# AdaLN modulation as one fp32 product on the array's column quarters, and the token mixers' two-operand elementwise work on VectorE

## The chip, the cores and the metric

The kernel runs on one core of a Trainium2 chip. The metric is the device time of one execution in microseconds (us). TensorE (PE in the profile) multiplies matrices, VectorE (DVE), ScalarE (ACT) and GpSimd (POOL) work on elements, and SyncE (SP) issues most DMA transfers. Each engine runs its instructions in the order in which they stand in its own queue.

## The reference

One layer of a hybrid decoder in fp32, on a prompt of 1024 tokens and 8 samples of 4 tokens. The conditioning vectors `c` (one for the prompt and one for each sample, nine in all) give scale, shift and gate of both sub-layers:

```
mod = silu(c) @ w_ada + b_ada                       # 1024 -> 6*1024, for 9 rows
sh1, sc1, gt1, sh2, sc2, gt2 = split(mod, 6)
h = rmsnorm(x, norm1) * (1 + sc1) + sh1
y = token_mixers(h)     # p = h @ w_in; RWKV-7 on p[:1792], HGRN2 on the rest; @ w_out
x = x + gt1 * y
h = rmsnorm(x, norm2) * (1 + sc2) + sh2
x = x + gt2 * (square(relu(h @ w_up)) @ w_down)
```

Among the elementwise work of the mixers are, in RWKV, `kk = k * k_k`, `k * (1 + (a-1) k_a)`, the bonus `sum(r * k * r_k) * v` and `+ lnx_b`.

## The kernel before

A matrix product in fp32 precision is made of three fp32r products. `load_w` brings a piece of a weight (`wraw`, 128x512), ACT copies it to fp32r (`whi`, L172), an elementwise engine subtracts that from the weight (`wlo`, L176), and `gemm` multiplies the high part of the weight by the high and the low part of the activation, and the low part by the high (L186 to L188). For the input projection L176 stands on DVE for 99 pieces and on POOL for 45; 96 more come back from DRAM as they were written at first use.

The stages, with their times in the profiled execution:

- **Opening, 0 to 55 us.** `x0`, the first quarter of the tokens with the samples (288 columns), is loaded and then the 8 halves of four blocks of `w_ada` (`wa`, 1 MB each), which give scale and shift of the first norm. `ada_block` splits each 128x512 piece on ACT (`wah`, L235) and DVE (`wal`, L236; two pieces on POOL) and multiplies it by `c_hl`, the split conditioning (L238, L239), into `ps_adb`. `adt` copies that out of PSUM, `two9` adds the halves and transposes (L244, `ps_ada`), and `mod` gets the bias. `modulate0` then scales and shifts `x0` (L306, L307, L310) and splits it into `h` and `l`.
- **Mixers, 55 to about 935 us.** 120 units of input projection, 24 matmuls each, evacuated into RWKV parts (`praw`, `xsh` by L585 to L591, sent to DRAM as `x_d`) or HGRN parts. Between them run nine RWKV groups (`rwkv`, three in flight at different steps), the HGRN heads (`hgrn_mix`), the norms of the other quarters (`sqa`, L264), and 16 calls of `ada_pair`, which make the rest of `mod`, two of its 48 pieces per call, in the way of `ada_block` (`wada`, `wahi` L214, `walo` L215, matmuls L218 and L219). About half of the pairs come in the last 85 us, when no projection is left.
- **Output projection and MLP, 935 to 1746 us.** POOL has nothing to do there.

In an RWKV group `X` is read back from `x_d`; L687 on POOL makes `kk` from it, and L690, L691 and L715 the other two-operand products. DVE makes `bo` in the same tile as `kk` (L720), four small DMAs of SP carry it into `bot`, and POOL adds `lnx_b` there (L727). The triangular inverse of the group is a chain of small steps on POOL (L825, L827), on `iat`, which comes back from DRAM.

A scheduler decides at build time, by its own estimates of durations, in which order each engine's instructions stand. A change of engines or instructions therefore reorders the mixers as a whole.

## Time and profile before

| | us |
|---|---|
| median of 3 runs (1748.58 to 1761.52) | 1751.42 |
| profiled execution | 1748.32 |
| its span, from the first instruction to the last | 1746.4 |
| PE busy | 1601.1 |
| DVE busy | 1277.9 |
| ACT busy | 903.4 |
| POOL busy | 466.7 |

The busy times are of the whole span. The stages have different limits, so what a change is worth is read stage by stage. POOL's whole work lies before 935 us.

### The profile page before, as it was taken

How to read it: one execution, taken by the hardware profiler on the slowest of the kernel's cores; microseconds unless marked ns; L12 is line 12 of the kernel's file. 1: busy time of each engine (PE TensorE's matmuls, PEld its weight loads, DVE VectorE, ACT ScalarE, POOL GpSimd, SP SyncE). 2: the span in 40 equal slices, each digit the busy share in tenths (PEclk: the TensorE clock that was granted, in tenths of full speed). 3: DMA queues.
4: the chain of work that ended last, by engine and by line, in shares of the span. 5: the costliest groups of instructions: out<-in, count | busy, mean ns of one | idle time of the engine just before them, and what ended most of it. 6: DMA issues, size and time to landing. Idle time of an engine off the chain costs nothing.

```text
span 1746.4 us, 38086 instructions
## 1 busy us (share of the span) xinstructions
PE 1601.1 (92%) x14224; PEld 1491.0 (85%) x14224; DVE 1277.9 (73%) x2735; ACT 903.4 (52%) x1861; POOL 466.7 (27%) x977
## 2 busy tenths in 40 slices
PE   6787998999899999899988997999999999999895
PEld 3777887787788888788867997999999999999895
DVE  7777878786655657566776669655655869798998
ACT  6446543446466665657654446455444554443351
POOL 3755738546351625436340000000000000000000
PEclk9899889999889999998988998999999999999997
DMA  7676675866677775765547533443333442324122
GB/s 261 191 226 220 200 231 155 289 211 186 180 230 219 217 227 167 220 183 156 160 143 250 202 129 116 142 140 102 105 104 111 154 147 94 111 87 139 35 75 100
DMA packets 216168, 288.66 MB, mean 165 GB/s; under 512 B 48264, under 2 KB 119304, under 8 KB 212912
## 3 DMA queue, kind: packets, MB, share of 16 engines
q1 hardware_dynamic: 198112, 263.16, 47.7%
q10 hardware_dynamic: 17776, 23.01, 3.9%
q8 instruction: 112, 1.84, 0.4%
q14 instruction: 72, 0.59, 0.1%
q0 software_dynamic: 96, 0.07, 0.0%
HBM read 225.64 MB, written 58.29 MB: 163 GB/s over the span
## 4 chain that ended last, share of the span: by engine, by line
PE 60%; DVE 17%; DMA 8%; ACT 5%; issue 4%; POOL 4%; SPq 1%; ACTq 0%; DVEq 0%; POOLq 0%
PE ps_g L1097 36%; PE ps_in L186 3%; PE ps_in L187 3%; PE ps_in L188 3%; DMA wraw<-w_in 2%; POOL itmp L825 2%; POOL ixt L827 2%; PE ps_A L755 1%; PE ps_l L429 1%; DVE acc L1384 1%; DMA x<-xT 1%; DVE wlo L1086 1%; DVE bl L1380 1%; DVE wlo L176 1%; DMA iat<-at_d 1%
## 5 line engine op out<-in xcount | busy, mean ns | idle before, releaser
L1097 PE MATMUL ps_g<-bh,whi 128*128 128x264 f32 x1792 | 370.7, 287 | 13.6 <-ACT whi L1085 8.5
L1097 PE MATMUL ps_g<-bh,wlo 128*128 128x264 f32 x1792 | 369.9, 287 | 9.0 <-DVE wlo L1086 9.0
L1097 PE MATMUL ps_g<-bl,whi 128*128 128x264 f32 x1792 | 371.0, 287 | 1.4 <-DVE bl L1380 1.4
L186 PE MATMUL ps_in<-h,whi 128*128 128x256 f32 (+1 forms) x960 | 292.2, 306 | 17.8 <-ACT psmp L583 8.4
L1097 PEld LDWEIGHTS ps_g<-bh,whi 128*128 128x128 f32 x1792 | 282.6, 190 | 14.6 <-ACT whi L1085 8.7
L1097 PEld LDWEIGHTS ps_g<-bh,wlo 128*128 128x128 f32 x1792 | 281.1, 190 | 9.7 <-DVE wlo L1086 9.7
L187 PE MATMUL ps_in<-l,whi 128*128 128x256 f32 (+1 forms) x960 | 286.7, 299 | 3.0 <-DVE l L1064 2.1
L188 PE MATMUL ps_in<-h,wlo 128*128 128x256 f32 (+1 forms) x960 | 285.7, 299 | 3.8 <-DVE wlo L176 3.7
L1097 PEld LDWEIGHTS ps_g<-bl,whi 128*128 128x128 f32 x1792 | 281.9, 190 | 1.6 <-DVE bl L1380 1.6
L186 PEld LDWEIGHTS ps_in<-h,whi 128*128 128x128 f32 x960 | 189.6, 198 | 32.2 <-ACT psmp L583 10.2
L172 ACT ACTIVATE whi<-wraw 128x512 fp32r<-128x512 f32 x240 | 147.6, 627 | 111.8 <-PE ps_in L187 55.9
L187 PEld LDWEIGHTS ps_in<-l,whi 128*128 128x128 f32 x960 | 190.2, 198 | 7.6 <-DVE l L1064 2.5
L188 PEld LDWEIGHTS ps_in<-h,wlo 128*128 128x128 f32 x960 | 189.4, 198 | 7.7 <-DVE wlo L176 4.8
L1085 ACT ACTIVATE whi<-wd 128x512 fp32r<-128x512 f32 x112 | 69.4, 630 | 163.9 <-PE ps_g L1097 127.5
L1085 ACT ACTIVATE whi<-wu 128x512 fp32r<-128x512 f32 x112 | 70.3, 632 | 145.6 <-PE ps_g L1097 140.2
L825 POOL TENSOR_TENSOR itmp<-ixt,iat 128x60 f32<-128x60 f32 (+24 forms) x248 | 92.0, 371 | 65.8 <-DMA iat<-at_d 49.4
L1086 DVE TENSOR_TENSOR wlo<-wu,whi 128x512 fp32r<-128x512 f32 x112 | 76.5, 687 | 39.3 <-ACT whi L1085 39.1
L176 DVE TENSOR_TENSOR wlo<-wraw,whi 128x512 fp32r<-128x512 f32 x99 | 77.4, 786 | 34.5 <-ACT whi L172 34.3
L827 POOL TENSOR_TENSOR ixt<-ixt,itmp 128x60 f32<-128x60 f32 (+24 forms) x248 | 90.3, 364 | 17.2
L1086 DVE TENSOR_TENSOR wlo<-wd,whi 128x512 fp32r<-128x512 f32 x112 | 76.0, 685 | 13.6 <-ACT whi L1085 13.5
L1380 DVE TENSOR_TENSOR bl<-u,bh 128x528 fp32r<-128x528 f32 x112 | 73.8, 702 | 2.3 <-ACT bh L1379 2.3
L176 POOL TENSOR_TENSOR wlo<-wraw,whi 128x512 fp32r<-128x512 f32 x45 | 60.7, 1352 | 25.8 <-ACT whi L172 19.8
(399 smaller groups left out, 3239.3 us busy)
## 6 DMA issues: line engine op xcount, KB each, us to landing
wraw<-w_in SPq DMA_DIRECT2D x240, 256.0 KB, 3.9
wlo<-wlo_d SPq DMA_DIRECT2D x96, 256.0 KB, 4.0
wu<-w_up SPq DMA_DIRECT2D x74, 256.0 KB, 2.8
u<-u_d SPq DMA_DIRECT2D x16, 1056.0 KB, 4.9
wada<-w_ada SPq DMA_DIRECT2D x64, 256.0 KB, 3.8
wd<-w_down SPq DMA_DIRECT2D x64, 256.0 KB, 2.6
u_d<-c SPq DMA_DIRECT2D x48, 264.0 KB, 3.0
wa<-w_ada SPq DMA_DIRECT2D x8, 1024.0 KB, 14.4
```

The source lines that it names most:

```text
L172: nc.scalar.activation(hi, raw, AF.Copy)
L176: eng[i].tensor_tensor(lo, raw, hi.bitcast(F32), op=ALU.subtract)
L186: nc.tensor.matmul(out, lhsT=wh, rhs=ah, start=first and k == 0, stop=False)
L187: nc.tensor.matmul(out, lhsT=wh, rhs=al, start=False, stop=False)
L188: nc.tensor.matmul(out, lhsT=wl, rhs=ah, start=False, stop=last and k == len(w) - 1)
L429: nc.tensor.matmul(ps[:, c, :], lhsT=z[:, cs], rhs=zc[:, :, 1, :], start=True, stop=True)
L825: G.tensor_tensor(tm, xt[:, 0:ns, j:j + 1].to_broadcast([P, ns, w]), at[:, j, j + 1:32].unsqueeze(1).to_broadcast([P, ns, w]), op=ALU.mult)
L827: G.tensor_tensor(dst, dst, tm, op=ALU.add)
L1085: self.nc.scalar.activation(hi, src, AF.Copy)
L1086: self.nc.vector.tensor_tensor(lo, src, hi.bitcast(F32), op=ALU.subtract)
L1097: nc.tensor.matmul(out[c], lhsT=w[x][:, k, :], rhs=a[y][:, k, c * 264:c * 264 + 264], start=first and k == 0 and j == 0, stop=last and k = ...
L1380: V.tensor_tensor(lo[:, k, :], src[:, k, :], hi[:, k, :].bitcast(F32), op=ALU.subtract)
```

## The change

It has two parts.

AdaLN: no split any more. The conditioning `c_silu` is padded with zeros from 9 to 32 columns, each piece of `w_ada` goes into one fp32 matmul as it comes from DRAM, and the product of input block `k` is written to PSUM partitions `32*(k%4)` and up, so that four blocks in turn use the four column quarters of the array. `ps_adb` and `ps_adp` so hold four partial sums, and `four9` (128x9) adds them while it transposes. The copies L235 and L214 and the subtractions L236 and L215 are gone, and with them the tiles `wah` and `wal`.

Elementwise work: fifteen kinds of two-operand instructions of the mixers and the opening go from POOL to DVE (among them the 45 subtractions of L176, `sqa`, L1630 on `x0`, and of an RWKV group L687, L690, L691, L715 and L727). The inverses, the sample part of `modulate0`, copies and memsets stay on POOL.

```diff
@@ -190,59 +187,48 @@
-        self.csr = pool.tile([P, KT, 2, NSEQ], F32R, name="c_hl")
-        nc.vector.tensor_copy(self.csr[:, :, 0, :], self.cs)
-        nc.vector.tensor_tensor(self.csr[:, :, 1, :], self.cs, self.csr[:, :, 0, :].bitcast(F32), op=ALU.subtract)
+        self.cs = pool.tile([P, KT, 32], F32, name="c_silu")
+        nc.vector.memset(self.cs, 0.0)
+        nc.vector.tensor_tensor(self.cs[:, :, 0:NSEQ], c, s, op=ALU.mult)
+
+    def ada_product(self, ps, k, w):
+
+        g = 32 * (k % 4)
+        self.nc.tensor.matmul(ps[g:g + 32], lhsT=self.cs[:, k, :], rhs=w, start=k < 4, stop=k >= KT - 4, skip_group_check=True)
+
+    def ada_mod(self, m, n, ps, pool, pp, tag):
+
+        nc = self.nc
+        t = pool.tile([P, n, P], F32, tag="adt", name="adt", bufs=1)
+        nc.scalar.activation(t, ps, AF.Copy)
+        for i in range(n):
+            ps = pp.tile([P, NSEQ], F32, tag=tag, name="ps_ada")
+            nc.tensor.matmul(ps, lhsT=t[:, i, :], rhs=self.four9, start=True, stop=True)
+            nc.vector.tensor_scalar(self.mod[:, m + i, :], ps, self.vec("b_ada", m + i), None, op0=ALU.add)
...
     def ada_pair(self, m, wpool, pool, pp, tag):
-        nc = self.nc
-        ps = pp.tile([2 * NSEQ, 2, P], F32, tag=tag, name="ps_adp")
+        ps = pp.tile([P, 2, P], F32, tag=tag, name="ps_adp")
         for k0 in range(0, KT, 2):
             raw = wpool.tile([P, 2, 2, P], F32, tag="wraw", name="wada", bufs=WB[0])
-            nc.sync.dma_start(raw, self.io["w_ada"][m:m + 2, :, k0:k0 + 2, :].rearrange("m p k c -> p m k c"))
-            hi = wpool.tile([P, 2, 2, P], F32R, tag="whi", name="wahi", bufs=WB[1])
-            lo = wpool.tile([P, 2, 2, P], F32R, tag="wlo", name="walo", bufs=WB[1])
-            nc.scalar.activation(hi, raw, AF.Copy)
-            nc.vector.tensor_tensor(lo, raw, hi.bitcast(F32), op=ALU.subtract)
+            self.nc.sync.dma_start(raw, self.io["w_ada"][m:m + 2, :, k0:k0 + 2, :].rearrange("m p k c -> p m k c"))
             for k in range(2):
-                c = self.csr[:, k0 + k]
-                nc.tensor.matmul(ps, lhsT=c.rearrange("p two s -> p (two s)"), rhs=hi[:, :, k, :], start=k0 + k == 0, stop=False)
-                nc.tensor.matmul(ps[:NSEQ], lhsT=c[:, 0, :], rhs=lo[:, :, k, :], start=False, stop=k0 + k == KT - 1)
+                self.ada_product(ps, k0 + k, raw[:, :, k, :])
+        self.ada_mod(m, 2, ps, pool, pp, tag)
...
     def ada_block(self, b, raw, pool, pg, ph):
 
-        nc = self.nc
-        ps = pg.tile([2 * NSEQ, 4, P], F32, tag="g", name="ps_adb")
-        for kh in range(2):
-            hi = pool.tile([P, 4, 4, P], F32R, tag="wah", name="wah", bufs=2)
-            lo = pool.tile([P, 4, 4, P], F32R, tag="wal", name="wal", bufs=2)
-            for k in range(4):
-                nc.scalar.activation(hi[:, :, k], raw[kh][:, :, k], AF.Copy)
-                (nc.gpsimd if b >= AB and k == AK else nc.vector).tensor_tensor(lo[:, :, k], raw[kh][:, :, k], hi[:, :, k].bitcast(F32), op=ALU.subtract)
-                c = self.csr[:, kh * 4 + k]
-                nc.tensor.matmul(ps, lhsT=c.rearrange("p two s -> p (two s)"), rhs=hi[:, :, k, :], start=kh == 0 and k == 0, stop=False)
-                nc.tensor.matmul(ps[:NSEQ], lhsT=c[:, 0, :], rhs=lo[:, :, k, :], start=False, stop=kh == 1 and k == 3)
+        ps = pg.tile([P, 4, P], F32, tag="g", name="ps_adb")
+        for k in range(KT):
+            self.ada_product(ps, k, raw[k // 4][:, :, k % 4, :])
+        self.ada_mod(4 * b, 4, ps, pool, ph, "h")
...
-        G.tensor_tensor(r, k, r, op=ALU.mult)
+        V.tensor_tensor(r, k, r, op=ALU.mult)
...
-                G.tensor_tensor(qs, qe[:, cols[j]].unsqueeze(1).to_broadcast([P, 4, SC]), self.tokm[:, gs, :], op=ALU.mult)
+                V.tensor_tensor(qs, qe[:, cols[j]].unsqueeze(1).to_broadcast([P, 4, SC]), self.tokm[:, gs, :], op=ALU.mult)
-                G.tensor_tensor(s0, s0, el[:, gs, :].to_broadcast([P, 4, P]), op=ALU.mult)
+                V.tensor_tensor(s0, s0, el[:, gs, :].to_broadcast([P, 4, P]), op=ALU.mult)
                 vm = pool.tile([SC, 4, P], F32, tag="hvm", name="hvm", bufs=B_hvm)
-                G.tensor_tensor(vm, vt[:, j, :].unsqueeze(1).to_broadcast([SC, 4, P]),
+                V.tensor_tensor(vm, vt[:, j, :].unsqueeze(1).to_broadcast([SC, 4, P]),
...
         kk = t4("kk")
-        G.tensor_tensor(kk, k, bc4(self.vec("k_k")), op=ALU.mult)
+        V.tensor_tensor(kk, k, bc4(self.vec("k_k")), op=ALU.mult)
...
-        G.tensor_tensor(k, k, cs, op=ALU.mult)
-        G.tensor_tensor(a, a, sg, op=ALU.mult)
+        V.tensor_tensor(k, k, cs, op=ALU.mult)
+        V.tensor_tensor(a, a, sg, op=ALU.mult)
...
-        G.tensor_tensor(cs, r, k, op=ALU.mult)
+        V.tensor_tensor(cs, r, k, op=ALU.mult)
         bo = kk
...
-        G.tensor_tensor(bt, bt, bc4(self.vec("lnx_b")), op=ALU.add)
+        V.tensor_tensor(bt, bt, bc4(self.vec("lnx_b")), op=ALU.add)
...
-                G.tensor_tensor(ax[:, j], ar[:, j, 0, y, :32].unsqueeze(1).to_broadcast([P, NS, 32]), self.tokm, op=ALU.mult)
+                V.tensor_tensor(ax[:, j], ar[:, j, 0, y, :32].unsqueeze(1).to_broadcast([P, NS, 32]), self.tokm, op=ALU.mult)
...
-                G.tensor_tensor(rm, R[:, j, h, :].unsqueeze(1).to_broadcast([P, NS, 64]),
+                V.tensor_tensor(rm, R[:, j, h, :].unsqueeze(1).to_broadcast([P, NS, 64]),
...
-            G.tensor_tensor(oc, oc, rs[:, c].unsqueeze(2).to_broadcast([P, 4, 64]), op=ALU.mult)
+            V.tensor_tensor(oc, oc, rs[:, c].unsqueeze(2).to_broadcast([P, 4, 64]), op=ALU.mult)
...
-                            self.square_add(hp, x(k), acc, k == 0, nc.gpsimd)
+                            self.square_add(hp, x(k), acc, k == 0, nc.vector)
...
-                    (nc.gpsimd if k in XM else nc.vector).tensor_tensor(x0[:, k, :], x0[:, k, :], r0, op=ALU.mult)
+                    nc.vector.tensor_tensor(x0[:, k, :], x0[:, k, :], r0, op=ALU.mult)
...
-                V, G = nc.vector, nc.gpsimd
-                w = self.load_w(wp, io["w_in"][m], wlo_d.get(m), m in seen, (V, V) if m in seen else [(G, G), (G, V)][self.nw % 2])
+                V = nc.vector
+                w = self.load_w(wp, io["w_in"][m], wlo_d.get(m), m in seen, (V, V))
...
-    o["two9"] = np.concatenate([np.eye(NSEQ, dtype=np.float32)] * 2)
+    o["two9"] = np.concatenate([np.eye(32, NSEQ, dtype=np.float32)] * 4)
```

The first place is PE's order at the end of the opening; `ps_adb` is the product with `w_ada`, `ps_ada` its transposition into `mod`, and `ps_in` the first unit of the projection. Before:

```order
L238 MATMUL ps_adb<-wah,c_hl 18x512
L239 MATMUL ps_adb<-wal,c_hl 9x512
L244 MATMUL ps_ada<-two_77,adt 128x9 x4
L186 MATMUL ps_in<-h_388,whi 128x288 x2
L187 MATMUL ps_in<-l_389,whi 128x288
L188 MATMUL ps_in<-h_388,wlo 128x288
```

Now:

```order
L213 MATMUL ps_ada<-four_74,adt 128x9 x2
L204 MATMUL ps_adb<-wa_138,c_silu 32x512 x4
L204 MATMUL ps_adb<-wa_141,c_silu 32x512 x4
L213 MATMUL ps_ada<-four_74,adt 128x9 x4
L204 MATMUL ps_adb<-wa_142,c_silu 32x512 x4
L213 MATMUL ps_ada<-four_74,adt 128x9 x4
L183 MATMUL ps_in<-h_273,whi 128x288
L184 MATMUL ps_in<-l_274,whi 128x288
```

The products with `wa` now stand in fours, one for each quarter, and wait for the load alone; the pairs that waited for ACT's copy and DVE's subtraction are gone.

The second place is an RWKV group in the middle of the mixers, where `bot` and the `kk` of the next group are made. Before, POOL's queue:

```order
L1014 TENSOR_TENSOR oc<-oc,ors 128x256 x2
L727 TENSOR_TENSOR bot<-bot,vecs 128x512
L687 TENSOR_TENSOR kk<-X,vecs 128x512
L438 TENSOR_TENSOR hr<-hk,hr 128x256
L383 MEMSET hr 128x128
L825 TENSOR_TENSOR itmp<-ixt,iat 128x31
```

Now DVE's queue (L706 is `bo`, L713 `bot`, L673 `kk`; the lines between them are of HGRN heads and of another group):

```order
L706 TENSOR_TENSOR kk<-X,ps_bo 128x512
L368 COPY hr<-hf 128x128
L373 TENSOR_TENSOR hf<-hf 128x128
L713 TENSOR_TENSOR bot<-bot,vecs 128x512
L438 SCALAR_TENSOR_TENSOR hst<-hst,hf,ps_s 128x128 x2
L350 TENSOR_SCALAR hf<-hsig,fs,fb 128x256
L365 TENSOR_TENSOR hz<-hq,hf 128x64x2
L371 TENSOR_TENSOR hz<-hk,hr 128x64x2
L372 TENSOR_TENSOR hr<-hr,hf 128x64x2
L744 TENSOR_TENSOR Aa<-ps_A,amask 128x256
```

The two instructions that wait for DMAs now stand in DVE's queue, `bot` two short instructions behind the `bo` that its DMAs carry, and `kk` some ten further on.

## Rows read from the trace of the kernel before

**Rows 1.** Windows by stage; after each bracket its length, busy times, clock, DMA.

```profile
core 0: us, PE busy (x) PEld busy (x) DVE busy (x) ACT busy (x) POOL busy (x), PEclk, DMA share, GB/s
0.00:55.00 55.00, 36.08 (x132) 18.87 (x133) 42.33 (x89) 31.82 (x66) 24.24 (x33) 0.84 0.66 232
55.00:112.00 57.00, 48.09 (x336) 45.87 (x335) 42.73 (x71) 23.12 (x60) 43.77 (x83) 0.97 0.63 192
112.00:400.00 288.00, 257.55 (x2101) 222.65 (x2099) 227.46 (x517) 144.03 (x345) 162.71 (x286) 0.94 0.71 224
400.00:850.00 450.00, 417.83 (x4559) 377.98 (x4559) 287.19 (x816) 275.02 (x614) 202.93 (x509) 0.94 0.66 197
850.00:935.00 85.00, 67.86 (x871) 54.80 (x869) 64.77 (x194) 50.70 (x121) 33.01 (x70) 0.88 0.52 156
935.00:1746.00 811.00, 773.67 (x6237) 770.84 (x6236) 613.45 (x1052) 378.75 (x656) 0.00 (x0) 0.97 0.36 122
```

**Rows 2.** Windows, 33 to 43 us, same columns.

```profile
33.00:43.00 10.00, 9.22 (x34) 3.60 (x33) 9.34 (x18) 6.00 (x12) 4.88 (x4) 0.78 0.01 3
```

**Rows 3.** Timeline of the opening: start, length, what [idle before, releaser].

```profile
42.29 0.59 ACT L241 ACTIVATE adt<-ps_adb 18x512 f32<-18x512 f32 x1 [0.33 <-PE ps_adb L239]
...
51.07 0.61 PE L187 MATMUL ps_in<-l,whi 128*128 128x288 f32 x1 [2.14 <-DVE l L1064]
```

**Rows 4.** Groups by line: busy us, mean ns of one | idle before them.

```profile
L176 DVE TENSOR_TENSOR wlo<-wraw,whi 128x512 fp32r<-128x512 f32 x99 | 77.4, 786 | 34.5 <-ACT whi L172 34.3
L1086 DVE TENSOR_TENSOR wlo<-wu,whi 128x512 fp32r<-128x512 f32 x112 | 76.5, 687 | 39.3 <-ACT whi L1085 39.1
L176 POOL TENSOR_TENSOR wlo<-wraw,whi 128x512 fp32r<-128x512 f32 x45 | 60.7, 1352 | 25.8 <-ACT whi L172 19.8 <-DMA wraw<-w_in 2.6 <-PE ps_in L188 2.3
L215 DVE TENSOR_TENSOR walo<-wada,wahi 128x512 fp32r<-128x512 f32 x64 | 46.3, 731 | 20.7 <-ACT wahi L214 20.1 <-ACT hkt L402 0.2
L214 ACT ACTIVATE wahi<-wada 128x512 fp32r<-128x512 f32 x64 | 39.4, 628 | 31.5 <-DMA wada<-w_ada 12.1 <-PE ps_in L187 11.5 <-PE ps_adp L218 3.7
L586 DVE SCALAR_TENSOR_TENSOR xsh<-dsh,vecs,praw 128x256 f32<-128x256 f32 x56 | 37.7, 673 | 0.6
```

**Rows 5.** Line L586 and line L825: duration in ns, min/median/max.

```profile
L586 DVE SCALAR_TENSOR_TENSOR xsh<-dsh,vecs,praw x56: 383/484/1557, 59.5 to 468.8; 128x256 f32<-128x256 f32 x56
...
L825 POOL TENSOR_TENSOR itmp<-ixt,iat x248: 202/308/1402, 254.7 to 893.4; 128x60 f32<-128x60 f32 x12, 128x54 f32<-128x54 f32 x8, 128x66 f32<-128x66 f32 x8, 128x28 f32<-128x28 f32 x8
```

**Rows 6.** PE's timeline: fp32r products of a pair, an fp32 matmul, fp32 on quarters.

```profile
164.53 0.28 PE L218 MATMUL ps_adp<-wahi,c_hl 128*18 128x256 f32 x1
164.65 0.28 PE L219 MATMUL ps_adp<-walo,c_hl 128*9 128x256 f32 x1
...
271.95 1.07 PE L996 MATMUL ps_Ss<-rm,btm 128*64 128x512 f32 x2
272.86 0.34 PE L422 MATMUL ps_l<-hz 128*64 128x64 f32 x3
...
300.54 0.25 PE L986 MATMUL ps_Os<-R,Ar 128*32 128x64 f32 x2
300.56 0.25 PE L981 MATMUL ps_Os<-R,Ar 128*32 128x64 f32 x2
...
300.64 0.23 PE L981 MATMUL ps_Os<-R,Ar 128*32 128x64 f32 x2
```

**Rows 7.** POOL's waits: us in total, times, longest.

```profile
POOL bot L727 <- DMA bot<-kk: 61.7, 8, 20.9
...
POOL kk L687 <- DMA X<-x_d: 21.0, 8, 6.0
```

**Rows 8.** Issues of the four bot DMAs in 400 to 850 us, and to landing.

```profile
L726 SPq DMA_DIRECT2D bot<-kk x24: 590/629/1101, 471.0 to 846.8; - x24
...
DMA to landing us min/median/max: 2.0/3.0/5.5
```

**Rows 9.** The chain of waits from 850 to 935 us, by line.

```profile
by line: POOL itmp L825 16.5%; POOL ixt L827 14.9%; issue 8.2%; PE ps_adp L218 4.1%; PE ps_adp L219 4.1%; DMA wo<-w_out 4.0%; DMA at_d<-Aa 3.7%; DMA iat<-at_d 3.3%; PE ps_ada L224 3.0%; PE ps_l L429 2.9%; DMA XT<-xt_d 2.5%; DMA xt_d<-ixt 2.
```

More of the change, by code (lines that the diff above doesn't have):

```diff
@@ L84 @@
 PSB = 2, 2, 1
-AK = 3
 LSQ = ()
@@ L90 @@
 HP0 = 1000
-AB = 3
-XM = (0, 1, 2, 3, 4, 5, 6, 7)
 EPS = 1e-6
@@ L151, in consts @@
         nc.gpsimd.dma_start(self.ident, io["ident"])
-        self.two9 = pool.tile([2 * NSEQ, NSEQ], F32, name="two9")
-        nc.gpsimd.dma_start(self.two9, io["two9"])
+        self.four9 = pool.tile([P, NSEQ], F32, name="four9")
+        nc.gpsimd.dma_start(self.four9, io["two9"])
         self.seqm = pool.tile([P, NS], F32, name="seqm")
@@ L192, in silu_c @@
         nc = self.nc
+        self.mod = pool.tile([P, 48, NSEQ], F32, name="mod")
         c = pool.tile([P, KT, NSEQ], F32, name="c_in")
         nc.scalar.dma_start(c, self.io["cT"])
-        s = pool.tile([P, KT, NSEQ], F32, name="c_sig")
+        s = self.mod[:, 0:KT, :]
         nc.scalar.activation(s, c, AF.Tanh, scale=0.5)
         nc.vector.tensor_scalar(s, s, 0.5, 0.5, op0=ALU.mult, op1=ALU.add)
-        self.cs = pool.tile([P, KT, NSEQ], F32, name="c_silu")
-        nc.vector.tensor_tensor(self.cs, c, s, op=ALU.mult)
@@ L200, in silu_c @@
-        self.csr = pool.tile([P, KT, 2, NSEQ], F32R, name="c_hl")
-        nc.vector.tensor_copy(self.csr[:, :, 0, :], self.cs)
-        nc.vector.tensor_tensor(self.csr[:, :, 1, :], self.cs, self.csr[:, :, 0, :].bitcast(F32), op=ALU.subtract)
-        self.mod = pool.tile([P, 48, NSEQ], F32, name="mod")
+        self.cs = pool.tile([P, KT, 32], F32, name="c_silu")
[4 more added lines that the diff above has]
+        self.nc.tensor.matmul(ps[g:g + 32], lhsT=self.cs[:, k, :], rhs=w, start=k < 4, stop=k >= KT - 4, skip_group_check=True)
@@ L220, in ada_pair @@
-        t = pool.tile([2 * NSEQ, 2, P], F32, tag="adt", name="adt", bufs=1)
-        nc.scalar.activation(t, ps, AF.Copy)
-        for i in range(2):
-            ps = pp.tile([P, NSEQ], F32, tag=tag, name="ps_ada")
-            nc.tensor.matmul(ps, lhsT=t[:, i, :], rhs=self.two9, start=True, stop=True)
-            nc.vector.tensor_scalar(self.mod[:, m + i, :], ps, self.vec("b_ada", m + i), None, op0=ALU.add)
-    def ada_block(self, b, raw, pool, pg, ph):
-        nc = self.nc
-        ps = pg.tile([2 * NSEQ, 4, P], F32, tag="g", name="ps_adb")
-        for kh in range(2):
-            hi = pool.tile([P, 4, 4, P], F32R, tag="wah", name="wah", bufs=2)
-            lo = pool.tile([P, 4, 4, P], F32R, tag="wal", name="wal", bufs=2)
-            for k in range(4):
-                nc.scalar.activation(hi[:, :, k], raw[kh][:, :, k], AF.Copy)
-                (nc.gpsimd if b >= AB and k == AK else nc.vector).tensor_tensor(lo[:, :, k], raw[kh][:, :, k], hi[:, :, k].bitcast(F32), op=ALU.subtract)
-                c = self.csr[:, kh * 4 + k]
-                nc.tensor.matmul(ps, lhsT=c.rearrange("p two s -> p (two s)"), rhs=hi[:, :, k, :], start=kh == 0 and k == 0, stop=False)
-                nc.tensor.matmul(ps[:NSEQ], lhsT=c[:, 0, :], rhs=lo[:, :, k, :], start=False, stop=kh == 1 and k == 3)
-        t = pool.tile([2 * NSEQ, 4, P], F32, tag="adt", name="adt", bufs=1)
-        nc.scalar.activation(t, ps, AF.Copy)
-        for m in range(4):
-            ps = ph.tile([P, NSEQ], F32, tag="h", name="ps_ada")
-            nc.tensor.matmul(ps, lhsT=t[:, m, :], rhs=self.two9, start=True, stop=True)
-            nc.vector.tensor_scalar(self.mod[:, 4 * b + m, :], ps, self.vec("b_ada", 4 * b + m), None, op0=ALU.add)
```

## The prediction

> **What bounds the kernel now.** The first view is the windows by stage [rows 1]. From 935 us on PE is busy 774 of 811 us, POOL not at all, and no line of the change runs there: that stage stays as it is. What can move lies in the first 935 us, and each stage there has its own limit. In the opening DVE is the fullest engine (42 of 55 us). In the first units (55 to 112 us) POOL has 44 of 57 us and DVE 43. From 112 to 400 us PE has 258 of 288 us, DVE 227, POOL 163. From 400 to 850 us PE has 418 of 450 us, and DVE, at 64%, isn't the bound. In the last 85 us no engine is full: the time is a chain. PE's busy time counts overlapping records, so there is slack behind it.
>
> The second view is the opening close up. From 33 to 43 us the DMA engines are idle (share 0.01) while DVE is busy 9.3 of 10 us [rows 2]: all of `wa` has landed and the split is what is being waited for. The last `ps_adb` is copied out at 42.29 us, and the first unit runs on from 51.07 us [rows 3].
>
> The third view is durations. The same subtraction of 128x512 takes 687 ns on DVE in the MLP, where POOL is silent, 786 ns in the mixers, and 1352 ns on POOL [rows 4]. L586 has a median of 484 ns, a mean of 673 and a longest of 1557 [rows 4, 5]; L825 on POOL runs from 202 to 1402 ns with a median of 308. Both engines stretch each other: some instructions wait a whole instruction of the other.
>
> **The change part by part.**
>
> *Opening.* The 32 copies on ACT and 32 subtractions go. After the last load (33 us at the latest) there remain one group of four fp32 products, then what follows 42.29 us today. An fp32 matmul of 512 columns takes some 0.91 us to the start of the next [rows 6]. That makes 33 + 1 + 8.8 (from 42.29 to 51.07) = 42.8 us for the first unit: 8 us gained, one end. The other: of those 8.8 us most is scaling, shifting and splitting both halves of `x0` on a DVE that POOL stretches, and the first half needs only the blocks that land before the last. If it is ready when the last `ps_ada` is, about 2 us behind the product, PE starts near 35 us: 16 us gained. The norm on `x0`, now on DVE, comes while the loads still run, and 8 instructions below 0.69 us are 5.5 us at most, under the loads. In SP's queue nine small constants now stand ahead of the first `w_in` pieces; their transfer falls into the stretch in which the DMA engines were idle, but the first `wraw` may come 2 to 3 us later than the product, so I take **-13** (-16 to -6).
>
> *First units, 55 to 112 us.* POOL, the fullest engine, gives its subtractions and squares to DVE at half the price each (687 against 1352). DVE gets about 16 us more and loses the stretch (L586's mean to its median is 28% of its time, so some 12 us of 43). **-3** (-8 to +3).
>
> *112 to 400 us.* Here DVE becomes the tight engine. Of POOL's 163 us I reckon about 100 as moved work (inverses begin only at 254.7 us [rows 5], and copies and memsets are small); at 687/1352 that is 51 us on DVE. It loses a share of its stretch, between the 13% of L176 (786 to 687) and the 28% of L586: 227 x 0.15 = 34, of which some two thirds go with the moved work, 22 us. So 227 + 51 - 22 = 256 of 288 us, 89% against 79%. If DVE keeps all its idle time of 61 us, the stage ends 29 us later; if that idle time was only waiting for others (PE is at 89% as well), it ends no later, and shorter steps of the groups gain up to 10. Nearer to the second, because DVE's largest wait at L176 is for ACT [rows 4], which gets no more work: **+6** (-10 to +25).
>
> *400 to 850 us.* About half of the 16 pairs are here. A pair has 16 fp32r matmuls at 0.12 us [rows 6], 1.9 us; now it has 8 fp32 matmuls of 256 columns, 0.46 us each if alone (half of 0.91), 0.46 for four if they run at once. That four run at once the trace shows: on four quarters the records of L986 and L981 start at 300.54 and 300.56 us and the second pass follows at 300.64 [rows 6], where four in series, at 64/512 of 0.91 us each, would need 0.46 us. So a pair costs 0.9 instead of 1.9 us, 16 us less in all sixteen, half of them here. ACT loses 39 us of copies in all [rows 4], DVE 46 of subtractions, of which half here; DVE gets back some 30 us of moved work. DVE stays near 64%, PE has 8 us less: **-5** (-12 to +30, for the wait in the first rival).
>
> The Trainium skill, "TensorEngine Tiling (Array Packing)", section Key Properties, says that switching the tiling mode drains the TensorEngine. In the rows a record of L218 lasts 0.28 us at a spacing of 0.12 [rows 6]; if each switch cost those 0.16 us, at both ends of some 45 runs of quarter matmuls, it would be 14 us of PE, and with half of it on the path the sum below would be 7 us nearer to zero. No row shows such a gap at a change of the columns, so I take nothing for it.
>
> *Last 85 us.* The chain of waits has 8.2% in L218 and L219 and 31.4% in the inverse on POOL [rows 9]. Half of the pairs stand here: their DVE and ACT work of about 20 us each goes. The chain's 7 us in L218 and L219 fall to half; the inverse, at 26.7 us on the chain, has less DVE beside it and may fall toward its median. What is late next is `at_d` and back, which stays. **-6** (-11 to 0).
>
> That the remaining POOL work gains is supported by the Trainium skill, "SBUF — State Buffer", section "SBUF: two separate sides": a VectorE instruction with two SBUF inputs and a GpSimd instruction that reads SBUF lock each other out for a whole instruction. The trace agrees (202 to 1402 ns at L825). By the same rule every moved instruction now holds up the inverses that stay, so the gain in the middle stage is less than POOL's relief.
>
> Sum: -13 - 3 + 6 - 5 - 6 = **-21**. Against the profiled execution of 1748.3 us (span 1746.4) that is 1727; the median of the runs is 3.1 us above it, so the forecast is **1730**.
>
> **The rivals.**
>
> *DVE's queue waits for DMAs.* `bot` (L713) and `kk` (L673) wait for transfers. On POOL that wait cost nobody: it sat 61.7 us before `bot` and 21.0 us before `kk` in eight waits each [rows 7]. In DVE's queue everything behind them waits too: HGRN steps, masks of the next group, subtractions for the projection, and with these PE. `bot` has four DMAs issued 0.63 us apart with a median of 3.0 us to landing [rows 8], some 4.9 us behind `bo`; the order puts two short instructions between in the place shown, some 2 us at most. That leaves about 3 us a group, and the 2.6 us a time of `kk` come on top: 5.6 x 6 late groups = 34 us if nothing hides it. With a middle stage at its bad end (+25 for +6) the time is 1730 + 34 + 19 = 1783; with half of the wait hidden and the middle at +6 it is 1747. It decides for slower when over two thirds of the wait are on the path and the middle stage is near its bad end. For it: DVE is near full up to 400 us. Against: from 400 us DVE has 160 us of idle time to absorb 34. Chance 0.22, centre 1757.
>
> *The quarters don't run at once.* Then a pair takes 8 x 0.46 = 3.7 us, against the forecast 2.8 us more, 44 us of PE in sixteen pairs. The last group of the opening takes 4 x 0.91 instead of 0.91, 3 us. With half of the 44 us on the path: 1730 + 22 + 3 = 1755. The rows of L986 speak against. Chance 0.10.
>
> *More is gained.* The opening counts fully (-16), the middle stage isn't held by DVE (-10), and shorter steps and less contention shorten the groups (-12, -8 first units, -6 tail): -52, 1700. For it: DVE's stretched instructions stand on the chains of the groups. Chance 0.18.
>
> **How the numbers follow.** Forecast 0.50, its own range 1715 to 1745. 1% (17.5 us) is about what a measurement of this kernel can tell from no change. Faster by over 1% is below 1734: 0.36 of the forecast's 0.50, and the 0.18 of the larger gain, 0.54. Within 1%: 0.14 of the forecast, 0.13 and 0.06 of the two slow rivals, 0.33. Slower: 0.13. The range reaches from the larger gain to the middle of the slow end: 1697 to 1768.
>
> **What would show it.** Right: the first unit starts between 35 and 43 us; four L204 records start within 0.1 us; DVE at 85 to 92% in the stage of the first norms, its subtraction near 700 ns; L811 (L825 before) near 308 ns; no wait of DVE for the DMAs of `bot` and `X` over 1 us a time. Wrong: long waits of DVE at L713 and L673 with idle PE behind them, L204 of the pairs in series at 0.46 us each, or a stage from 112 us on that takes longer than 300 us.

## The result and the profile after

| | us |
|---|---|
| median before, 4 runs (1748.58 to 1761.52) | 1750.91 |
| median after, 4 runs (1700.30 to 1711.84) | 1705.81 |
| ratio, with its 95% interval | 0.9739 [0.9703, 0.9775] |
| profiled execution after | 1707.11 |
| its span | 1705.3 |

The changed kernel is 45 us faster; 21 were forecast. The windows by stage of the changed kernel, cut as in [rows 1] (start, end, length, busy times, clock, DMA share, GB/s):

```profile
0.00:55.00 55.00, 40.28 (x202) 27.07 (x203) 29.09 (x95) 22.60 (x50) 9.36 (x33) 0.78 0.87 295
55.00:112.00 57.00, 56.03 (x433) 55.25 (x432) 48.06 (x133) 33.77 (x86) 15.62 (x46) 1.00 0.81 261
112.00:400.00 288.00, 265.44 (x2295) 227.71 (x2295) 225.97 (x585) 146.22 (x341) 108.80 (x256) 0.91 0.68 211
400.00:850.00 450.00, 423.48 (x4670) 374.43 (x4668) 282.40 (x887) 264.43 (x595) 143.76 (x448) 0.94 0.65 197
850.00:935.00 85.00, 76.89 (x728) 64.17 (x722) 51.25 (x141) 33.77 (x73) 0.00 (x0) 0.86 0.75 250
935.00:1705.00 770.00, 731.02 (x5917) 728.71 (x5915) 585.80 (x994) 360.75 (x625) 0.00 (x0) 0.98 0.34 113
```

The cuts fall on other work now, but one thing is plain: between 55 and 112 us PE is busy 56 of 57 us, where it was 48, at a granted clock of 1.00 (0.97 before). POOL went from 44 to 16 us there, and yet DVE did more, 48 for 43.

The right cuts are events. I take the first copy of a projection unit out of PSUM by ACT (the first evacuation; L581 before, L567 now), the 14th, which ends the first RWKV part, the last projection matmul, and the first matmul of the output projection:

| | before | after | measured | forecast |
|---|---|---|---|---|
| start to first evacuation | 58.0 | 47.4 | -10.6 | -13 |
| to the 14th evacuation | 54.3 | 41.6 | -12.7 | -3 |
| to the last projection matmul | 738.3 | 731.1 | -7.2 | +1 (6 - 5) |
| to the first output projection matmul | 83.2 | 70.1 | -13.1 | -6 |
| to the end, with what lies outside the span | 814.5 | 816.9 | +2.4 | 0 |
| profiled execution | 1748.3 | 1707.1 | -41.2 | -21 |

The opening, in the timeline of the changed kernel (start, length, what):

```profile
30.61 1.94 PE L204 MATMUL ps_adb<-wa,c_silu 128*32 128x512 f32 x8
...
32.67 0.60 ACT L210 ACTIVATE adt<-ps_adb 128x512 f32<-128x512 f32 x1 [5.95 <-PE ps_adb L204]
...
35.46 0.61 PE L183 MATMUL ps_in<-h,whi 128*128 128x288 f32 x1
```

The last `ps_adb` is copied at 32.67 us for 42.29 [rows 3], and the projection begins at 35.46 us: within the forecast 35 to 43. (That is the start of the first matmul, which came at 48.08 us before; the prediction set it against 51.07, where the unit ran on after a wait. The first evacuation is the fairer mark.) The eight records of L204 are four fp32 matmuls, one on each quarter.

The first units are where the forecast failed most plainly. Here are the groups of the kernel before between its first and 13th evacuation (58 to 108 us; busy us, mean ns of one | idle before it), a stretch that the prediction didn't look at by itself:

```profile
58.00:108.00 50.00, 41.09 (x282) 38.87 (x281) 37.89 (x62) 20.45 (x56) 38.78 (x72) 0.97 0.60 181
...
L186 PE MATMUL ps_in<-h,whi 128*128 128x288 f32 x93 | 29.1, 312 | 8.4 <-ACT psmp L583 8.4
L188 PE MATMUL ps_in<-h,wlo 128*128 128x288 f32 x93 | 28.2, 303 | 0.0
L176 POOL TENSOR_TENSOR wlo<-wraw,whi 128x512 fp32r<-128x512 f32 x19 | 25.9, 1365 | 4.9 <-ACT whi L172 4.8
L586 DVE SCALAR_TENSOR_TENSOR xsh<-dsh,vecs,praw 128x256 f32<-128x256 f32 x12 | 10.7, 891 | 0.1
L591 DVE SCALAR_TENSOR_TENSOR xsh<-dsmp,vecs,psmp 128x32 f32<-128x32 f32 x12 | 8.1, 676 | 0.1
L585 DVE TENSOR_TENSOR dsh<-praw 128x256 f32<-128x256 f32 x12 | 7.3, 612 | 7.6 <-ACT praw L581 7.6
L590 DVE TENSOR_TENSOR dsmp<-psmp 128x32 f32<-128x32 f32 x12 | 4.9, 409 | 0.1
```

And the same units of the changed kernel, 47.4 to 86 us:

```profile
47.40:86.00 38.60, 37.98 (x273) 37.58 (x273) 31.19 (x80) 21.11 (x54) 15.45 (x48) 0.96 0.69 215
...
L572 DVE SCALAR_TENSOR_TENSOR xsh<-dsh,vecs,praw 128x256 f32<-128x256 f32 x12 | 5.8, 482 | 0.1
L577 DVE SCALAR_TENSOR_TENSOR xsh<-dsmp,vecs,psmp 128x32 f32<-128x32 f32 x12 | 2.9, 245 | 0.0
L571 DVE TENSOR_TENSOR dsh<-praw 128x256 f32<-128x256 f32 x12 | 5.0, 420 | 3.0 <-ACT praw L567 3.0
L576 DVE TENSOR_TENSOR dsmp<-psmp 128x32 f32<-128x32 f32 x12 | 2.2, 185 | 0.0
```

The four DVE steps of a unit took 891 + 676 + 612 + 409 = 2588 ns, now 482 + 245 + 420 + 185 = 1332. The step on 32 columns (L591) needs 245 ns and took 676 on average. Its twelve records show why: the five that ran beside one of POOL's subtractions took 1244 to 1347 ns, about as long as such a subtraction (1365), and the seven others 237 to 252. PE waited for the evacuation (`psmp`, 8.4 us) and never for a `wlo` that POOL delivered late: L188, which reads it, has no idle time before it. DVE now does 24 subtractions there instead of 5 and is still less busy (31.2 for 37.9 us). The 50 us became 38.6, of which PE is busy 37.98: this stage is now bound by the projection itself. The chain of waits in the same two stretches, by line, before and after:

```profile
by line: issue 19.8%; DVE xsh L591 14.1%; DVE xsh L586 10.3%; PE ps_in L186 7.7%; PE ps_in L187 6.2%; DVE dsmp L590 6.1%; PE ps_in L188 5.9%; DVE dsh L585 5.9%; ACTq L593 5.3%; ACT praw L581 5.3%; ACT whi L172 4.5%; DVE rkb L618 3.8%; DVE m
```

```profile
by line: PE ps_in L183 33.8%; PE ps_in L184 32.0%; PE ps_in L185 31.8%; ACT praw L567 1.7%; ACT psmp L569 0.5%; issue 0.3%
```

The four DVE steps held 36% of the chain and PE's products 20%; now the products are 98% of it.

The waits of DVE's queue for DMAs that the first rival counted, in the whole span (us, times, longest):

```profile
DVE bot L713 <- DMA bot<-kk: 16.3, 6, 6.2
...
DVE kk L673 <- DMA X<-x_d: 9.1, 5, 2.6
```

They came, 25 us in all, at up to 6.2 and 2.6 us a time, where I had named less than 1 us as the sign of a right forecast.

In the tail, from the last projection matmul to the output projection, the chain of waits by line (820 to 890 us) has no inverse in it any more (before: [rows 9]):

```profile
by line: PE ps_adp L204 19.1%; DMA wada<-w_ada 17.7%; DMA wo<-w_out 9.1%; PE ps_l L415 7.8%; PE ps_SA L893 3.6%; PE ps_ada L213 3.3%; PE ps_g L1010 3.2%; PE ps_O L889 3.1%; PE ps_O L910 2.7%; PE ps_d L396 2.6%; PE ps_U L882 2.6%; PE ps_oT L
```

The last inverse runs from 815 to 838 us, at the start of the tail; before it ran from 862 to 894 of 851 to 934 us. Its steps are hardly shorter: L811 has a median of 302 ns and a mean of 353, where L825 had 308 and 371.

### The profile page after: what moved, and what is told of

It is laid out like the page before. It is cut to its first block, busy times and chain, and to the rows that moved or that the text cites. A ratio compares the mean times of both kernels' runs of the same rounds, so it can differ in the third digit from the quotient of the medians.

```text
span 1705.3 us, 37741 instructions
## 1 busy us (share of the span) xinstructions
PE 1593.1 (93%) x14224; PEld 1477.3 (87%) x14224; DVE 1222.6 (72%) x2832; ACT 861.5 (51%) x1767; POOL 277.6 (16%) x783
## 3 DMA queue, kind: packets, MB, share of 16 engines
q8 instruction: 112, 1.84, 0.4%
## 4 chain that ended last, share of the span: by engine, by line
PE 65%; DVE 12%; DMA 9%; POOL 5%; ACT 4%; issue 3%; SPq 2%; DVEq 0%; ACTq 0%; POOLq 0%
PE ps_g L1083 35%; PE ps_in L183 5%; PE ps_in L185 5%; PE ps_in L184 5%; DMA wraw<-w_in 2%; POOL ixt L813 2%; PE ps_l L415 2%; PE ps_A L741 2%; POOL itmp L811 2%; DVE acc L1370 1%; PE ps_adp L204 1%; DVE bl L1366 1%; DVE wlo L1072 1%; DVE x L1109 1%; DMA iat<-at_d 1%
## 5 line engine op out<-in xcount | busy, mean ns | idle before, releaser
L173 DVE TENSOR_TENSOR wlo<-wraw,whi 128x512 fp32r<-128x512 f32 x144 | 99.0, 690 | 25.4 <-ACT whi L169 24.5
L811 POOL TENSOR_TENSOR itmp<-ixt,iat 128x60 f32<-128x60 f32 (+24 forms) x248 | 87.6, 353 | 121.2 <-DMA iat<-at_d 103.5
L1365 ACT ACTIVATE bh<-u 128x528 fp32r<-128x528 f32 x112 | 62.8, 632 | 0.0
```

The costliest lines, as they stand in the source:

```text
L173: eng[i].tensor_tensor(lo, raw, hi.bitcast(F32), op=ALU.subtract)
L811: G.tensor_tensor(tm, xt[:, 0:ns, j:j + 1].to_broadcast([P, ns, w]), at[:, j, j + 1:32].unsqueeze(1).to_broadcast([P, ns, w]), op=ALU.mult)
L1365: A(hi[:, k, :], src[:, k, :], AF.Copy)
```

## The experiments

Each variant is built anew, so the scheduler's order differs in all of them. The table has the median, the ratio to the kernel before on the same chip with its interval, and from the profiled execution the first evacuation, the time from it to the 13th, the 14th evacuation, and the time from there to the last instruction, all in us. These last four come from one execution each, and the runs of one variant differ by 7 to 24 us.

| kernel | median | ratio | first | 1st to 13th | 14th | behind it |
|---|---|---|---|---|---|---|
| before | 1750.9 | | 58.0 | 49.6 | 112.3 | 1630 |
| after | 1705.8 | 0.9739 [0.9703, 0.9775] | 47.4 | 38.5 | 89.0 | 1612 |
| e_ada | 1737.6 | 0.9929 [0.9892, 0.9966] | 49.0 | 49.3 | 103.1 | 1637 |
| e_move | 1764.9 | 1.0068 [1.0034, 1.0102] | 55.6 | 37.5 | 96.3 | 1659 |
| e_lo | 1736.6 | 0.9912 [0.9880, 0.9944] | 57.5 | 40.5 | 101.2 | 1629 |
| e_loG | 1722.8 | 0.9802 [0.9723, 0.9881] | 51.1 | 48.6 | 104.5 | 1615 |
| e_dD0 | 1726.2 | 0.9864 [0.9791, 0.9938] | 47.6 | 39.5 | 90.2 | 1627 |
| e_restG | 1711.1 | 0.9761 [0.9699, 0.9824] | 46.2 | 37.4 | 86.9 | 1611 |
| e_ser | 1747.0 | 0.9961 [0.9926, 0.9996] | 59.0 | 38.9 | 101.1 | 1627 |
| e_cpy | 1767.2 | 1.0092 [1.0063, 1.0122] | 59.0 | 46.3 | 110.1 | 1648 |
| e_psmp2 | 1752.6 | 1.0001 [0.9958, 1.0043] | 59.1 | 49.1 | 112.9 | 1631 |
| e_btkk | 1730.2 | 0.9882 [0.9846, 0.9917] | 47.9 | 38.5 | 89.6 | 1641 |
| e_nullA | 1713.1 | 0.9782 [0.9715, 0.9848] | 47.3 | 38.6 | 89.1 | 1615 |
| e_nullA4 | 1714.2 | 0.9778 [0.9736, 0.9819] | 47.5 | 38.4 | 89.0 | 1622 |
| e_nullA7 | 1732.6 | 0.9886 [0.9844, 0.9929] | 47.6 | 37.2 | 88.8 | 1636 |
| e_nullB | 1780.8 | 1.0156 [1.0090, 1.0222] | 59.2 | 49.7 | 112.0 | 1666 |
| e_nullB4 | 1771.6 | 1.0114 [1.0065, 1.0163] | 57.9 | 49.6 | 112.0 | 1662 |
| e_nullB7 | 1773.4 | 1.0131 [1.0086, 1.0177] | 59.0 | 48.9 | 114.2 | 1663 |
| e_split5 | 1733.2 | 0.9898 [0.9841, 0.9956] | 47.3 | 38.7 | 89.1 | 1641 |
| e_split6 | 1734.3 | 0.9899 [0.9868, 0.9929] | 47.0 | 39.0 | 89.1 | 1641 |

**e_ada**: the diff's hunks of `silu_c`, `ada_pair`, `ada_block` and the constants alone; the fifteen moved kinds stay on POOL.

```diff
-                nc.tensor.matmul(ps, lhsT=c.rearrange("p two s -> p (two s)"), rhs=hi[:, :, k, :], start=k0 + k == 0, stop=False)
-                nc.tensor.matmul(ps[:NSEQ], lhsT=c[:, 0, :], rhs=lo[:, :, k, :], start=False, stop=k0 + k == KT - 1)
+                self.ada_product(ps, k0 + k, raw[:, :, k, :])
...
```

> The AdaLN part alone: products in fp32 on the quarters, every elementwise instruction where it was before. Theory 1 (the first units were held by POOL's 1352 ns subtractions, which stretch the short DVE steps of a unit's evacuation): the opening gains its 10 us and the last 85 us some 6, the first units stay slow. From the first to the thirteenth evacuation of the projection 48 to 51 us as before (38.5 in the changed kernel). Time 1726 to 1738. Theory 2 (the first units run faster because ACT, DVE and the weight buffers are free of the AdaLN split): these thirteen evacuations in 38 to 42 us, time 1712 to 1722.

Theory 1 holds for the opening, which gains 9 us, and for the first units, which stay at 49.3. It doesn't for the tail, which takes 82 us for 83, where some 6 less were expected. The total is at the upper end of its range.

**e_move**: the other hunks alone.

```diff
-        G.tensor_tensor(kk, k, bc4(self.vec("k_k")), op=ALU.mult)
+        V.tensor_tensor(kk, k, bc4(self.vec("k_k")), op=ALU.mult)
...
```

> The moves from POOL to DVE alone, AdaLN split as before. Theory 1: the first unit comes no earlier than before (56 to 59 us), the thirteen evacuations take 38 to 42 us, and the stage of the first HGRN heads keeps its gain. Time 1722 to 1734. Theory 2: thirteen evacuations in 46 us or more, time 1740 to 1755.

The first units do as theory 1 says (37.5), and the 14th evacuation is 16 us early. But 29 us are lost behind it, and the whole is slower than before: neither theory has that. The two parts alone, -12 and +15, don't add up to -45.

**e_lo**: of the moves, the subtraction of the projection's weights alone, on the kernel before.

```diff
-                w = self.load_w(wp, io["w_in"][m], wlo_d.get(m), m in seen, (V, V) if m in seen else [(G, G), (G, V)][self.nw % 2])
+                w = self.load_w(wp, io["w_in"][m], wlo_d.get(m), m in seen, (V, V))
```

> The kernel before, with only the 45 subtractions of the w_in pieces moved from POOL to DVE. Theory 1: they alone free the first units, thirteen evacuations in 38 to 43 us, and give most of what the moves give: 1728 to 1740. Theory 2, or the view that every moved kind counts by its POOL time (61 of some 210 us): 1742 to 1753, and thirteen evacuations in 45 us or more.

Theory 1: 40.5 us for the units. Their steps are short again. Groups by line, 57.5 to 98 us:

```profile
L176 DVE TENSOR_TENSOR wlo<-wraw,whi 128x512 fp32r<-128x512 f32 x23 | 16.5, 718 | 5.0 <-ACT whi L172 5.0
L586 DVE SCALAR_TENSOR_TENSOR xsh<-dsh,vecs,praw 128x256 f32<-128x256 f32 x12 | 5.7, 472 | 0.1
L591 DVE SCALAR_TENSOR_TENSOR xsh<-dsmp,vecs,psmp 128x32 f32<-128x32 f32 x12 | 3.4, 285 | 0.0
```

**e_loG**: the reverse of that edit, on the changed kernel.

```diff
-                w = self.load_w(wp, io["w_in"][m], wlo_d.get(m), m in seen, (V, V))
+                w = self.load_w(wp, io["w_in"][m], wlo_d.get(m), m in seen, (V, V) if m in seen else [(G, G), (G, V)][self.nw % 2])
```

> The changed kernel, with the subtractions of the w_in pieces back on POOL. Theory 1: thirteen evacuations in 46 to 50 us, time 1716 to 1728, 10 to 22 us above the changed kernel. Theory 2: 40 us at most, time within 6 us of the changed kernel (1703 to 1712).

Theory 1: the units are back at 48.6 us and the time, by the medians, at +17. The intervals of the two ratios overlap, and orders alone move the time by as much (below). What counts here is the 14th evacuation, 15.5 us later (104.5 for 89.0); in the four orders of the changed kernel it stays between 88.8 and 89.1.

**e_dD0**: in `ada_pair` of the changed kernel, for each piece

```diff
+            z = wpool.tile([P, 2, 2, P], F32R, tag="wlo", name="waz", bufs=WB[1])
+            self.nc.vector.tensor_tensor(z, raw, raw, op=ALU.subtract)
```

> The changed kernel, with a subtraction on DVE for each of the 64 pieces of the sixteen pairs put back, into a tile of the wlo buffers that nobody reads (46 us of DVE before; no ACT copy, the product stays fp32 on the quarters). Theory 3 (VectorE has no room for the moved work and the split at once, so the moves pay only because the split goes): 1722 to 1740, most of it lost where the pairs stand. Theory 4 (a rebuilt order moves the time by itself, and that makes most of the difference between the sum of the parts, about +3, and the whole, -44): 1700 to 1718.

20 us above the changed kernel, as theory 3 has it, 15 of them behind the 14th evacuation. But e_nullA7 below loses more there by its order alone, so this run by itself tells little.

**e_restG**: the changed kernel with POOL again in all moves but that of `load_in`.

```diff
-        V.tensor_tensor(kk, k, bc4(self.vec("k_k")), op=ALU.mult)
+        G.tensor_tensor(kk, k, bc4(self.vec("k_k")), op=ALU.mult)
...
```

> The changed kernel with all other moved kinds back on POOL; of the moves only the 45 subtractions of the w_in pieces are left (AdaLN in fp32 on the quarters). If the parts add, -12 and -13 on the kernel before: 1720 to 1730. Theory 3, with room on VectorE made by the AdaLN part: more than the sum, 1708 to 1720, the thirteen first evacuations in 38 to 41 us.

1711 us, within the intervals of the changed kernel: once the 45 subtractions have moved, the other fourteen kinds of moved instructions give nothing that can be measured. Without them it may be otherwise: e_loG, with the fourteen, is 15 us faster than e_ada, without (one order each). No version beats the changed kernel clearly; this one equals it.

**e_nullA**: in the changed kernel

```diff
-NORM0 = 5
+NORM0 = 6
```

> The changed kernel with the norms of the later quarters begun one projection unit later (the sixth for the fifth): the same work, another order on every engine. It measures what a rebuilt order does by itself. Theory 3: within 6 us of the changed kernel (1700 to 1712). Theory 4: 8 to 25 us away from it on either side.

7 us slower by the medians, between the two theories; the intervals overlap.

**e_ser**: in `ada_product`, with `ps`, `adt` and `four9` cut to 32 partitions

```diff
-        g = 32 * (k % 4)
-        self.nc.tensor.matmul(ps[g:g + 32], lhsT=self.cs[:, k, :], rhs=w, start=k < 4, stop=k >= KT - 4, skip_group_check=True)
+        self.nc.tensor.matmul(ps, lhsT=self.cs[:, k, :], rhs=w, start=k == 0, stop=k == KT - 1)
```

> The changed kernel with all eight products of a pair or block accumulated on the first 32 partitions, so that the quarters don't work side by side. A pair's products then take some 3.7 us for 1.0. If PE's time in the pairs is on the path: 1720 to 1740; if it lies beside other waits: 1703 to 1714.

41 us lost by the medians, more than either case (the profiled execution in the table is its fastest, 1733.6). PE's timeline of the changed kernel, eight matmuls of a pair, and of this one, four:

```profile
865.45 1.07 PE L204 MATMUL ps_adp<-wada,c_silu 128*32 128x256 f32 x16
866.45 0.66 PE L415 MATMUL ps_l<-hz 128*128 128x64 f32 x4
```

```profile
871.67 1.91 PE L203 MATMUL ps_adp<-wada,c_silu 128*32 128x256 f32 x8
873.51 0.66 PE L414 MATMUL ps_l<-hz 128*128 128x64 f32 x4
```

To the start of the next product eight take 1.00 us and four 1.84 (each is two records): the quarters do work side by side, 3.7 times as fast. In the opening more than the whole gain of 10.6 us is lost (59.0 for 47.4), where the second rival of the prediction had 3.

**e_cpy**: the kernel before, with four copies in `rwkv_project` on ACT.

```diff
-        G.tensor_copy(shift_sb[:, m, 0:1], raw[:, np_:np_ + 1])
+        S.activation(shift_sb[:, m, 0:1], raw[:, np_:np_ + 1], AF.Copy)
...
```

> The kernel before, with the four small copies of each RWKV projection unit (shift_sb and the edge columns of praw and psmp) moved from POOL to ACT; the 45 subtractions stay on POOL. Theory 5a (POOL's long instructions stretch the DVE steps of the evacuation): the thirteen first evacuations still take 47 to 50 us, time 1743 to 1758. Theory 5b (the copies queue behind POOL's 1352 ns subtractions and hold the evacuation): 39 to 43 us, time 1730 to 1742.

46.3 us, by 5a and just under its range; L591 still takes 841 ns on average between the first and the 13th evacuation. So the copies behind POOL's subtractions held the units for 3 us at most. The whole is 15 us slower; whether by ACT's work or by the order isn't known.

```profile
L176 POOL TENSOR_TENSOR wlo<-wraw,whi 128x512 fp32r<-128x512 f32 x18 | 24.6, 1369 | 11.1 <-ACT whi L172 10.9
L591 DVE SCALAR_TENSOR_TENSOR xsh<-dsmp,vecs,psmp 128x32 f32<-128x32 f32 x12 | 10.1, 841 | 0.0
```

**e_psmp2**: the kernel before with

```diff
-B_psmp = 1
+B_psmp = 2
...
-B_dsmp = 1
+B_dsmp = 2
```

> The kernel before with two buffers instead of one for psmp and dsmp (and the conditioning's temporary kept in mod, to make room), so that the copy of a unit's sample columns out of PSUM needn't wait for the DVE steps of the unit before. Theory 5c (PE waits 8.4 us in these units because that copy waits for the one buffer): thirteen evacuations in 40 to 44 us, time 1733 to 1744. Theory 5a: the DVE steps themselves are too long, another buffer only shifts the wait: 46 to 50 us, time 1743 to 1758.

The units take 49.1 us, as before. PE's wait for `psmp` falls from 8.4 to 5.7 us, but ACT's next copy into `praw` waits 6.4 us for L591, where it was 3.5: the wait moves, as 5a says.

**e_btkk**: the changed kernel with `bot` (L713) and `kk` (L673) back on POOL.

```diff
-        V.tensor_tensor(kk, k, bc4(self.vec("k_k")), op=ALU.mult)
+        G.tensor_tensor(kk, k, bc4(self.vec("k_k")), op=ALU.mult)
...
-        V.tensor_tensor(bt, bt, bc4(self.vec("lnx_b")), op=ALU.add)
+        G.tensor_tensor(bt, bt, bc4(self.vec("lnx_b")), op=ALU.add)
```

> The changed kernel with bot and kk, the two instructions that wait for DMAs, back on POOL. If their 25 us of waiting in DVE's queue lie on the path (the first rival of the prediction): 1682 to 1697. If other work hides them: within the spread of rebuilt orders, 1698 to 1716.

24 us slower, against both readings, all of it behind the 14th evacuation. That the waits in DVE's queue cost 25 us is not borne out; how much of the loss is the new order can't be told from one run.

**e_nullB**: the edit of e_nullA in the kernel before.

> The kernel before with the norms of the later quarters begun one projection unit later: the same work in another order, as was done to the changed kernel. If a rebuilt order moves the time by some 7 us as there: 1742 to 1760. If by much more, differences of 10 us between variants say nothing: beyond 1735 or 1766.

28 us slower, beyond the 1766 that I had set: the kernel before stands in an order that suits it. From here on single variants that differ by 10 or 20 us behind the 14th evacuation prove nothing, so two more orders of each kernel follow.

**e_nullA4, e_nullA7, e_nullB4, e_nullB7**: `NORM0` 4 and 7 in both.

> The changed kernel with the norms of the later quarters begun one projection unit earlier (the fourth). Behind the 14th evacuation it takes 1612 us to the end of the span in the changed kernel, 1630 in the kernel before, 1615 and 1666 in the variants with the sixth unit. If the lighter queues make the gain there (6a): 1605 to 1625 behind that point, 1698 to 1718 in all. If it is chance of the order (6b): spread over 1612 to 1666, as likely above 1635 as below.

> The changed kernel with these norms begun at the seventh unit. 6a: 1605 to 1625 us behind the 14th evacuation, 1698 to 1718 in all. 6b: as likely above 1635 as below.

> The kernel before with these norms begun at the fourth unit. 6a: 1630 to 1670 us behind the 14th evacuation, above every variant of the changed kernel, 1745 to 1785 in all. 6b: as likely below 1625 as above.

> The kernel before with these norms begun at the seventh unit. 6a: 1630 to 1670 us behind the 14th evacuation, 1745 to 1785 in all. 6b: as likely below 1625 as above.

Three of the four as 6a says; e_nullA7 (1636) is above its range. With equal `NORM0` (4, 5, 6, 7) the changed kernel is faster behind the 14th evacuation by 39, 18, 51 and 27 us. The pair that was shown, with 5, is the smallest of the four there; by the medians of whole runs the changed kernel is faster by 57, 45, 68 and 41 us.

The orders tell the two halves of the gain apart. Up to the 14th evacuation it is 23 to 25 us in all four. Behind it the place of the gain depends on the order (profiled executions, us):

| `NORM0` | 14th to last projection matmul, before | after | from there to the output projection, before | after |
|---|---|---|---|---|
| 4 | 773.4 | 719.6 | 79.7 | 93.4 |
| 5 (shown) | 738.3 | 731.1 | 83.2 | 70.1 |
| 6 | 770.2 | 721.6 | 88.8 | 83.5 |
| 7 | 767.4 | 749.2 | 85.5 | 79.2 |

The two together are shorter by 40, 20, 54 and 25 us. The tail alone gains 13 us in the pair shown, 5 and 6 in two others, and loses 14 in the fourth.

**e_split5, e_split6**: the split's load without its use, in `ada_pair` of the changed kernel (6: with `NORM0 = 6`).

```diff
+            hi = wpool.tile([P, 2, 2, P], F32R, tag="whi", name="wahi", bufs=WB[1])
+            lo = wpool.tile([P, 2, 2, P], F32R, tag="wlo", name="walo", bufs=WB[1])
+            self.nc.scalar.activation(hi, raw, AF.Copy)
+            self.nc.vector.tensor_tensor(lo, raw, hi.bitcast(F32), op=ALU.subtract)
```

> The changed kernel with the copy on ACT and the subtraction on DVE of the sixteen pairs put back into the whi and wlo buffers, as in the kernel before, but read by nobody; the products stay in fp32 on the quarters. 7a (the split's load on ACT and VectorE, and its buffers, made the kernel before slower behind the 14th evacuation): 1635 to 1665 us there, 1724 to 1755 in all. 7b (the products on PE made it): 1612 to 1632, 1705 to 1722 in all.

> The same with the norms of the later quarters begun at the sixth unit. 7a: 1635 to 1670 us behind the 14th evacuation, against 1615 with the same begin and no split and 1666 in the kernel before. 7b: 1612 to 1632.

7a, in both orders: 1641 and 1641 against 1612 and 1615. The tail, where no projection is left, takes 105 and 106 us for 70 and 83; before it e_split5 is 8 us faster and e_split6 2 us slower. Windows from the last projection matmul to the output projection, of the changed kernel and of e_split5:

```profile
820.00:890.00 70.00, 59.08 (x759) 40.15 (x758) 40.20 (x155) 26.13 (x75) 14.86 (x49) 0.87 0.51 153
```

```profile
812.00:918.00 106.00, 77.00 (x972) 57.85 (x972) 74.53 (x228) 56.70 (x132) 25.62 (x64) 0.79 0.46 139
```

There e_split5's DVE has 34 us more work, its ACT 31; the last inverse starts at 851 us, for 815. Its chain by line has the inverse in front again, as in the kernel before [rows 9]:

```profile
by line: POOL itmp L815 12.2%; POOL ixt L817 11.9%; issue 8.9%; PE ps_adp L204 4.6%; DMA wada<-w_ada 4.0%; DMA at_d<-Aa 3.2%; DMA XT<-xt_d 2.9%; DMA iat<-at_d 2.8%; DMA bot<-kk 2.7%; DVE wlo L1076 2.6%; SPq L821 2.3%; PE ps_oT L1006 2.2%; P
```

## Why the prediction was right and wrong

Of the 20 us by which the profiled execution fell below the forecast sum, 10 lie in the first units and 15 behind them; the opening and the MLP give back 2.4 each.

*Opening, -13.* Right in kind and size: -10.6. The AdaLN part alone makes it (e_ada, -9.0), and it takes both, no split and the quarters: unsplit products in series give nothing (e_ser).

*First units, -3 (-8 to +3).* This is the step that failed: -12.7 measured. I gave DVE "about 16 us more" and took off 12 us of stretch, a sum of busy times, and so a small difference. What set the pace was the chain of one unit, PSUM copy, four short DVE steps, the next copy, and each step of it could wait for a whole POOL subtraction, as the twelve records of L591 show. The rows for it stood in the trace (L586 and its longest of 1557 ns [rows 5]), but I spread the stretch over DVE's total instead of reading it on the chain. Moved to DVE, the subtractions come between the chains, at half their length, and the steps keep to 239 to 252 ns (L577, which was L591). e_lo, e_loG, e_ada and e_move show that these 45 instructions do it and AdaLN doesn't; e_cpy leaves 3 us at most to POOL's queue, and e_psmp2 nothing to the single buffer.

*112 to 400 us, +6, and 400 to 850, -5.* Together +1 forecast, -7.2 measured, inside the ranges; over the four orders it is -7 to -54. That DVE would become the tight engine (89%) is not seen: from 112 to 400 us it is busy 226 of 288 us (78%), as before. The stretch that goes was mis-sized: I took off 34 us in all, 12 in the first units and 22 here. The 1473 DVE instructions that both kernels have in equal number before the output projection take 608 us by their records before and 535 now, 73 less; by the same records the moved work adds some 107 and the split's subtractions took some 72. e_move, where the split stays, loses 29 us behind the first units against the kernel before; since other orders alone do as much, that this is a full DVE is argued, not shown.

*Last 85 us, -6.* -13.1 measured in the pair shown, but -5, -6 and +14 with the other orders: the size belongs to the order, and how near it came to the range (-11 to 0) is luck. What recurs is that all behind the 14th evacuation is shorter by 18 to 51 us, where -5 was forecast (6 - 5 - 6). There the term for the split was mis-sized: I took a few us of PE and of the inverse. e_split5 and e_split6 put the split's load back, with the fast products kept, and lose 29 and 26 us, 35 and 23 in the tail. There nine pairs' copies and subtractions stand in ACT's and DVE's queues beside the last RWKV group, and its inverse comes late. That the same load made the kernel before slower is not shown: e_ada takes it away from that kernel and is no faster behind the 14th evacuation (1637 for 1630), and its tail takes 82 us for 83.

*Terms taken at nothing or for sure.* For the change of tiling I took nothing, as "no row shows such a gap". The records do show one, some 0.09 us each time (last section), before and after. That the remaining POOL work gains is hardly seen: the inverse's steps at L811 are 5% shorter on average.

*The rivals.* The quarters work side by side; the price that I set for the other case (+25) was too low, e_ser lost 41. DVE's queue did wait for DMAs, 25 us for the 34 that I had reckoned, but moving the two instructions back made the kernel slower: no run shows that price on the path, and one order can't rule it out. "More is gained" (1700) named the effect that decided in the first units, contention on the chains, and was given 0.18; its -8 there is nearer to the measured -12.7, its -16 for the opening is too much.

*What stays open.* How much of the gain behind the 14th evacuation belongs to which part. Over four orders it is 18 to 51 us. Variants with the AdaLN part and a part of the moves have it (e_restG 1611, e_loG 1615), e_ada doesn't (1637), and these are one order each. Why the kernel before is 32 to 36 us faster there in its given order than in three neighbours, nearly all of it before the last projection matmul, wasn't looked into.
